# An encoder layer on one core: w_out computed by token, its two groups summed apart, the residual kept by token from the first stage on

## The chip, the cores and the metric

The kernel runs on one core of a Trainium2 chip. The metric is the device time of one execution in microseconds (us); lower is better. A core has TensorE (PE in the profile), VectorE (DVE), ScalarE (ACT), GpSimd (POOL) and SyncE (SP), which here only issues DMAs. Each engine works through its own instructions in order; semaphores tie them together. Matrix products go into PSUM, everything else lives in SBUF.

## What is computed

One layer over 256 tokens of width 2048, all in float32:

```python
h = rmsnorm(x, norm1_g);  z = h @ w_in            # columns [u | v | B | C | h_B], 1024 each
u, v = gelu(z_u), gelu(z_v);  v = layernorm(v)
y_a = u * (masked w_spatial @ v + b)              # per head, in blocks of 128 tokens
y_b = B * causal_depthwise_conv3(C * h_B)
y = concat(rmsnorm(y_a, g[:1024]), rmsnorm(y_b, g[1024:]))
x = x + y @ w_out
h2 = rmsnorm(x, norm2_g)
x = x + (silu(h2 @ w_gate) * (h2 @ w_up)) @ w_down
return rmsnorm(x, final_norm_g)
```

The width of the inner layer is 5632.

## The kernel before

**Weights.** All weights stream through once, in units of 128 x 2048 floats (1 MB), each in two halves. SP issues the DMA of a half into `raw` (`load_unit`, L105). `split` then makes two parts of it for TensorE's fast float32 form: ScalarE casts `whi<-raw` (L86), VectorE takes the rest, `wlo<-raw,whi` (L87). There are five buffers for `raw` and four for each part, so up to two units are split ahead. The activations are split in the same way, with their gain (`split_scaled`, L171 and L172), and each product is made of three terms: high x high, low x high, high x low.

**Two forms of matmul.** By token (`mm_tok`, L128 to L130): the activations are the stationary operand, 512 weight columns stream, three matmuls per token block; the result has tokens in its partitions. By feature (`mm_feat`, L136 and L137): the weights are stationary and the activations stream, high and low part side by side in one matmul of 512 columns, and a second one of 256 columns for the low weights; the result has features in its partitions, in two halves that `sum_halves` adds.

**Stages**, in the order in which PE runs them, named by their accumulators: `v` (8 units, by token), `ch` (16, by feature), `u` (8, by feature), `b` (8, by feature), `o` for w_out (16, by feature), `gu` for gate and up (88, by token), `d` for down (44, by token). x arrives by feature in `xr` (`xk(k)` is its 128 features k) and stays so. The 1/rms of norm 1 is not applied to x but afterwards, to each stage's result.

**Norms.** A row sum over features is made from squares (ScalarE) that VectorE adds up (`add_squares`), then summed over partitions by small matmuls with ones (`rstd_tokens`, `ps_n`, `ps_na`, `ps_nb`), and raised to -1/2 on GpSimd (`rstd_of`). Where the factor is needed by feature it is laid on a diagonal and spread by a further matmul (`diagonal`, `spread`: `ps_n1b`, `ps_nab`, `ps_nbb`). Groups A and B of y are scaled by theirs (`norm_group`) before they are split into `yT`. So w_out sums both groups in one accumulator; its first three accumulators take group A's half first.

**Residual.** `out_pair` adds w_out's result to `xr` by feature and splits it into `hT`. During the first eight groups of `gu`, `residual` transposes it on PE (`ps_x`) into `x_tok`, by token, which the updates of `d` (`x2_of`, L534 and L536) and the final norm need.

**The order of the work** on each engine is not that of the program text: a planner fixes it when the program is built, by the order of the text and by its own estimate of when each instruction can start. On the chip each engine then keeps to that order. A DMA also waits for an earlier one whose semaphore it takes over; there are eight in turn.

**The first loads.** SP issues `head` (the gains and x's first 128 features), then the pieces of the first unit, in quarters of 256 KB, with x's loads between them (`first_x`, `load_x`). The first quarter goes out on ScalarE's queue. While they arrive, PE runs eight matmuls on ones (`ps_warm`).

Of the kernel before, what the change touches and what calls it, by code (L numbers as in the profile page):

```python
# [16 lines left out]
P = 128  # L17
# [14 lines left out]
def trunk_layer_kernel(  # L32
# [3 lines left out]
):  # L36

# [58 lines left out]
    def load_unit(piece=HU, between=None):  # L96
# [3 lines left out]
        for h in range(2):  # L100
            raw, hi, lo = half_tiles()
            for a in range(0, HU, piece):
                s = slice(a, a + piece)
                eng = nc.scalar if first_x is between and h + a == 0 else nc.sync
                eng.dma_start(raw[:, s], u[:, h * HU + a:h * HU + a + piece])  # L105
                if between is not None:
                    between((h * HU + a) // piece)
                split(hi[:, s], lo[:, s], raw[:, s])
# [104 lines left out]
    def add_squares(acc, y, first, name):  # L213
# [3 lines left out]
        if first:  # L217
            nc.vector.tensor_tensor(acc, sq[:, 0, :], sq[:, 1, :], op=ALU.add)
        else:
            for j in range(2):  # L220
                nc.vector.tensor_tensor(acc, acc, sq[:, j, :], op=ALU.add)
# [6 lines left out]
    warm = small.tile([P, 1], F32, tag="sf", name="warm")  # L228

# [4 lines left out]
    NA = 3  # L234
    queue(w_o, [2 * i for i in range(NA)] + [2 * i + 1 for i in range(NA)] + list(range(2 * NA, KD)))
# [22 lines left out]
    def first_x(i):  # L258
        if i == 0:
            nc.scalar.copy(warm, mhalf[:, 0:1])  # L260
            nc.gpsimd.tensor_copy(xk(0), head[:, NV:])
            split_scaled(xg[0], 0, head[:, NV:], vcol(G1, 0))
        elif i == 1:
            load_x(1, 1)
# [15 lines left out]
    xsq = row("xsq")  # L280
# [24 lines left out]
    for u in range(nv):  # L305
# [13 lines left out]
        add_squares(xsq, xk(2 * u, 2), u == 0, "x")  # L319
# [12 lines left out]
    def stat_x():  # L332
        nonlocal r1, r1s, dg1
        r1 = rstd_tokens(xsq, 1.0 / D, RMS_EPS, "n1")
# [68 lines left out]
    yA = bigtile([P, KA, T], F32, "yA")  # L403
    sqA = row("sqA")
    for k in range(0, KA, 2):
# [7 lines left out]
        nc.vector.tensor_tensor(yA[:, k:k + 2, :], z, mixT[:, k:k + 2, :], op=ALU.mult)  # L413
        add_squares(sqA, yA[:, k:k + 2, :], k == 0, "ya")

    yT = units_of(2 * CA, "yT")

    def norm_group(y, rb, base):
        for k in range(0, KA, 2):
            nc.vector.tensor_tensor(y[:, k:k + 2, :], y[:, k:k + 2, :], both(rb), op=ALU.mult)  # L420
            for j in range(2):
                kk = base + k + j
                split_scaled(yT[kk // KU], kk % KU, y[:, k + j, :], vcol(GG, kk))
# [3 lines left out]
    ra, rb = [], []  # L427
    for k in range(0, KA, 2):

        acc = gemm_feat(xg, "b", (lambda: ra.append(diagonal(rstd_tokens(sqA, 1.0 / AW, 4.0 * RMS_EPS, "na"), "na")))  # L430
                        if k == 2 else None)
        z = sum_halves(acc, "b")
        if k == 2:
            rab = spread(ra[0], "na")
# [235 lines left out]
```

## Time and profile before

| | us |
|---|---|
| runs | 1074.86, 1074.89, 1075.47 (median 1074.89) |
| profiled execution | 1074.51 |
| its span | 1072.7 |
| PE busy | 1058.9 (99% of the span) |
| VectorE busy | 627.7 (59%) |
| ScalarE busy | 491.9 (46%) |
| GpSimd busy | 5.8 (1%) |
| DMA | 205 MB, 191 GB/s over the span |

The span is what the trace covers; the profiled execution's time has some 1.8 us more around it. An engine is busy while an instruction of its own runs. Matmuls are pipelined: a new one starts every 0.2 us or so although each lasts 0.4, so the distance between starts tells what one costs, not its duration. The views of the trace that are used below: busy time by stage (windows), waits (who waited for whom), the chain of work that ended last, groups of instructions by line and shape, and the order in time of single engines.

### The profile page before, as it was taken

How to read it: one execution, taken by the hardware profiler on the slowest of the kernel's cores; microseconds unless marked ns; L12 is line 12 of the kernel's file. 1: busy time of each engine (PE TensorE's matmuls, PEld its weight loads, DVE VectorE, ACT ScalarE, POOL GpSimd, SP SyncE). 2: the span in 40 equal slices, each digit the busy share in tenths (PEclk: the TensorE clock that was granted, in tenths of full speed). 3: DMA queues.
4: the chain of work that ended last, by engine and by line, in shares of the span. 5: the costliest groups of instructions: out<-in, count | busy, mean ns of one | idle time of the engine just before them, and what ended most of it. 6: DMA issues, size and time to landing. Idle time of an engine off the chain costs nothing.

```text
span 1072.7 us, 13182 instructions
## 1 busy us (share of the span) xinstructions
PE 1058.9 (99%) x5086; PEld 888.5 (83%) x5086; DVE 627.7 (59%) x760; ACT 491.9 (46%) x598; POOL 5.8 (1%) x14
## 2 busy tenths in 40 slices
PE   7999999999999999999999999999999999999996
PEld 6888888888888888888888888888888888888885
DVE  7588667778766555555455555555555445454543
ACT  7464335565554544444444444444444334343432
POOL 0000000000000000000000000000000000000000
PEclk9999999999999999999999999999999999999999
DMA  9855555555555555555555555555556555555552
GB/s 325 270 186 178 176 177 188 186 183 182 184 193 181 190 182 182 191 185 186 184 191 195 182 191 191 184 195 189 183 196 223 191 194 196 194 195 188 194 191 79
DMA packets 58415, 205.25 MB, mean 191 GB/s; under 512 B 6960, under 2 KB 7216, under 8 KB 58224
## 3 DMA queue, kind: packets, MB, share of 16 engines
q1 hardware_dynamic: 57024, 201.13, 55.9%
q10 hardware_dynamic: 1328, 3.28, 1.0%
q8 instruction: 40, 0.66, 0.2%
q14 instruction: 23, 0.19, 0.0%
HBM read 202.28 MB, written 2.10 MB: 191 GB/s over the span
## 4 chain that ended last, share of the span: by engine, by line
PE 98%; issue 1%; DMA 0%; SPq 0%; ACT 0%; DVE 0%; POOLq 0%; POOL 0%; DVEq 0%
PE gu L128 15%; PE gu L130 15%; PE gu L129 15%; PE d L129 7%; PE d L128 7%; PE d L130 7%; PE o L136 6%; PE ch L136 6%; PE o L137 3%; PE ch L137 3%; PE u L136 3%; PE b L136 3%; PE v L128 1%; PE v L129 1%; PE b L137 1%; PE u L137 1%
## 5 line engine op out<-in xcount | busy, mean ns | idle before, releaser
L87 DVE TENSOR_TENSOR wlo<-raw,whi 128x1024 fp32r<-128x1024 f32 (+1 forms) x380 | 460.7, 1213 | 414.7 <-ACT whi L86 414.2
L86 ACT CAST whi<-raw 128x1024 fp32r<-128x1024 f32 (+1 forms) x380 | 395.6, 1041 | 557.8 <-PE gu L129 275.2
L128 PE MATMUL gu<-whi,hT 128*128 128x512 f32 x704 | 276.9, 393 | 0.0
L130 PE MATMUL gu<-wlo,hT 128*128 128x512 f32 x704 | 274.4, 390 | 0.0
L129 PE MATMUL gu<-whi,hT 128*128 128x512 f32 x704 | 273.9, 389 | 0.0
L130 PEld LDWEIGHTS gu<-wlo,hT 128*128 128x128 f32 x704 | 132.1, 188 | 28.0
L129 PEld LDWEIGHTS gu<-whi,hT 128*128 128x128 f32 x704 | 132.3, 188 | 26.6
L128 PEld LDWEIGHTS gu<-whi,hT 128*128 128x128 f32 x704 | 132.2, 188 | 26.5
L128 PE MATMUL d<-whi,aT 128*128 128x512 f32 x352 | 137.0, 389 | 0.0
L130 PE MATMUL d<-wlo,aT 128*128 128x512 f32 x352 | 136.9, 389 | 0.0
L129 PE MATMUL d<-whi,aT 128*128 128x512 f32 x352 | 136.9, 389 | 0.0
L136 PE MATMUL ch<-xg,whi 128*128 128x512 f32 x256 | 90.7, 399 | 0.0
L136 PE MATMUL o<-yT,whi 128*128 128x512 f32 x256 | 90.7, 399 | 0.0
L130 PEld LDWEIGHTS d<-wlo,aT 128*128 128x128 f32 x352 | 66.1, 188 | 13.8
L128 PEld LDWEIGHTS d<-whi,aT 128*128 128x128 f32 x352 | 66.1, 188 | 13.8
L129 PEld LDWEIGHTS d<-whi,aT 128*128 128x128 f32 x352 | 66.1, 188 | 13.5
L137 PE MATMUL o<-yT,wlo 128*128 128x256 f32 x256 | 71.9, 281 | 0.0
L137 PE MATMUL ch<-xg,wlo 128*128 128x256 f32 x256 | 71.7, 280 | 0.0
L136 PEld LDWEIGHTS o<-yT,whi 128*128 128x128 f32 x256 | 48.1, 188 | 11.8
L136 PEld LDWEIGHTS ch<-xg,whi 128*128 128x128 f32 x256 | 48.1, 188 | 11.5
L137 PEld LDWEIGHTS o<-yT,wlo 128*128 128x128 f32 x256 | 48.4, 189 | 0.0
L137 PEld LDWEIGHTS ch<-xg,wlo 128*128 128x128 f32 x256 | 48.3, 189 | 0.1
(137 smaller groups left out, 735.2 us busy)
## 6 DMA issues: line engine op xcount, KB each, us to landing
raw<-in_w_gu SPq DMA_DIRECT2D x176, 512.0 KB, 3.6
raw<-in_w_d SPq DMA_DIRECT2D x88, 512.0 KB, 4.3
raw<-in_w_ch SPq DMA_DIRECT2D x32, 512.0 KB, 3.6
raw<-in_w_o SPq DMA_DIRECT2D x32, 512.0 KB, 4.4
raw<-in_w_u SPq DMA_DIRECT2D x16, 512.0 KB, 3.6
raw<-in_w_b SPq DMA_DIRECT2D x16, 512.0 KB, 3.4
raw<-in_w_v SPq DMA_DIRECT2D x12, 512.0 KB, 6.4
out<-x_tok SPq DMA_DIRECT2D x8, 256.0 KB, 2.6
```

The costliest lines, as they stand in the source:

```text
L86: nc.scalar.copy(dst_hi, src)
L87: nc.vector.tensor_tensor(dst_lo, src, dst_hi.bitcast(F32), op=ALU.subtract)
L128: nc.tensor.matmul(acc, lhsT=ah, rhs=wh, start=first, stop=False)
L129: nc.tensor.matmul(acc, lhsT=al, rhs=wh, start=False, stop=False)
L130: nc.tensor.matmul(acc, lhsT=ah, rhs=wl, start=False, stop=last)
L136: nc.tensor.matmul(acc, lhsT=wh, rhs=at[:, kk, :, :], start=first, stop=False)
L137: nc.tensor.matmul(acc[:, 0:T], lhsT=wl, rhs=at[:, kk, 0, :], start=False, stop=last)
```

## The change

1. **w_out by token.** `w_o` is laid out for the form by token. Its 2048 columns are four chunks of 512, and each chunk is computed in two parts, one for group A and one for group B, each in its own accumulator of two units; the order is A of chunks 0 and 1, B of chunks 0 and 1, then A and B of chunks 2 and 3.
2. **1/rms in the update.** y of both groups goes into `yT` without its 1/rms (`y_out`), as soon as a pair of features is done. The factor, one per token and group, is applied when a part's accumulator is added to `x_tok`. `norm_group` and two spreads go away.
3. **Residual by token from `v` on.** After every second unit of `v`, `by_token` transposes a chunk of x on PE into `x_tok`: VectorE copies it out of PSUM, ScalarE squares it there with a sum along the row (`square_part`). `residual` goes away. After w_out's update x1 is transposed back (`x1_by_feature`) and split into `hT`, after the first unit of a following part, or of `gu` for the last chunk.
4. **Row sums.** Those of x and of x1 come from `square_part` and a short sum on VectorE (`rstd_parts`), without PE. The adds of the squares of y go to GpSimd.
5. **First loads.** SP issues all of them, so the first quarter of the first unit stands behind `head`; x's first further load follows it. The copy that makes ScalarE load its table (`warm`) moves to the top.

```diff
--- before.py
+++ after.py
@@ -101,8 +103,7 @@
             raw, hi, lo = half_tiles()
             for a in range(0, HU, piece):
                 s = slice(a, a + piece)
-                eng = nc.scalar if first_x is between and h + a == 0 else nc.sync
-                eng.dma_start(raw[:, s], u[:, h * HU + a:h * HU + a + piece])
+                nc.sync.dma_start(raw[:, s], u[:, h * HU + a:h * HU + a + piece])
                 if between is not None:
                     between((h * HU + a) // piece)
                 split(hi[:, s], lo[:, s], raw[:, s])
@@ -215,10 +216,21 @@
         sq = pair(F32, "b", f"sq_{name}")
         nc.scalar.activation(sq, y, AF.Square)
         if first:
-            nc.vector.tensor_tensor(acc, sq[:, 0, :], sq[:, 1, :], op=ALU.add)
+            nc.gpsimd.tensor_tensor(acc, sq[:, 0, :], sq[:, 1, :], op=ALU.add)
         else:
             for j in range(2):
-                nc.vector.tensor_tensor(acc, acc, sq[:, j, :], op=ALU.add)
+                nc.gpsimd.tensor_tensor(acc, acc, sq[:, j, :], op=ALU.add)
+
+    def rstd_parts(parts, eps, name):
+
+        ssum = small.tile([P, NT], F32, tag="rsp", name=f"{name}_s")
+        nc.vector.tensor_reduce(ssum, parts, axis=mybir.AxisListType.X, op=ALU.add)
+        return rstd_of(ssum, 1.0, eps, name)
+
+    def square_part(dst, src):
+
+        junk = tmp.tile([P, NW], F32, tag="b", name="jk")
+        nc.scalar.activation(junk, src, AF.Square, scale=D ** -0.5, accum_out=dst)
 
 
     mhalf = const.tile([P, 2], F32, name="mhalf")
@@ -226,13 +238,15 @@
     ones = const.tile([P, P], F32, name="ones")
     nc.vector.memset(ones, 1.0)
     warm = small.tile([P, 1], F32, tag="sf", name="warm")
+    nc.scalar.copy(warm, mhalf[:, 0:1])
 
     queue(w_v)
     queue(w_ch)
     queue(w_u)
     queue(w_b)
-    NA = 3
-    queue(w_o, [2 * i for i in range(NA)] + [2 * i + 1 for i in range(NA)] + list(range(2 * NA, KD)))
+
+    o_parts = [(0, 0), (1, 0), (0, 1), (1, 1)] + [(c, h) for c in range(2, NC) for h in range(2)]
+    queue(w_o, [c * NC + 2 * h + i for c, h in o_parts for i in range(2)])
     queue(w_gu)
     queue(w_d)
 
@@ -257,11 +271,9 @@
 
     def first_x(i):
         if i == 0:
-            nc.scalar.copy(warm, mhalf[:, 0:1])
+            load_x(1, 1)
             nc.gpsimd.tensor_copy(xk(0), head[:, NV:])
             split_scaled(xg[0], 0, head[:, NV:], vcol(G1, 0))
-        elif i == 1:
-            load_x(1, 1)
         elif i == 2:
             load_x(2, 2)
             split_scaled(xg[0], 1, xk(1), vcol(G1, 1))
@@ -277,7 +289,20 @@
     make_identity(nc, ident)
 
 
-    xsq = row("xsq")
+    x_tok = const.tile([P, NT, D], F32, name="x_tok")
+    ssx = const.tile([P, NT, NC], F32, name="ssx")
+    ss1 = const.tile([P, NT, NC], F32, name="ss1")
+
+    def by_token(c):
+
+        for t in range(NT):
+            ps = pmisc.tile([P, KU, P], F32, tag="pm", name="ps_x")
+            for k in range(KU):
+                nc.tensor.transpose(out=ps[:, k, :], in_=xk(c * KU + k)[:, t * P:(t + 1) * P], identity=ident)
+            ps = ps.rearrange("p k f -> p (k f)")
+            nc.vector.tensor_copy(x_tok[:, t, c * NW:(c + 1) * NW], ps)
+            square_part(ssx[:, t, c:c + 1], ps)
+
     r1 = r1s = dg1 = r1b = r1q = None
 
     def gelu2(acc, t, dst, name):
@@ -316,7 +341,8 @@
                 for t in range(NT):
                     mm_tok(vaccs[c][:, t, :], xg[u // 2], (2 * u + k) % KU, t, w[k], c,
                            u == 0 and k == 0, u == nv - 1 and k == 1)
-        add_squares(xsq, xk(2 * u, 2), u == 0, "x")
+        if u % 2 == 1:
+            by_token(u // 2)
 
 
     wsT = bigtile([P, H, P], F32, "wsT")
@@ -331,7 +357,7 @@
 
     def stat_x():
         nonlocal r1, r1s, dg1
-        r1 = rstd_tokens(xsq, 1.0 / D, RMS_EPS, "n1")
+        r1 = rstd_parts(ssx, RMS_EPS, "n1")
         r1s = const.tile([P, NT], F32, name="r1s")
         nc.vector.tensor_scalar(r1s, r1, GELU_S, None, op0=ALU.mult)
         dg1 = diagonal(r1, "n1")
@@ -400,8 +426,15 @@
             mix(2 * (k - (KA - H // 2)))
 
 
-    yA = bigtile([P, KA, T], F32, "yA")
+    yT = units_of(2 * CA, "yT")
     sqA = row("sqA")
+
+    def y_out(y, k, acc, name):
+
+        add_squares(acc, y, k % KA == 0, name)
+        for j in range(2):
+            split_scaled(yT[(k + j) // KU], (k + j) % KU, y[:, j, :], vcol(GG, k + j))
+
     for k in range(0, KA, 2):
         z = sum_halves(gemm_feat(xg, "u"), "u")
         nc.vector.tensor_tensor(z, z, both(r1b), op=ALU.mult)
@@ -410,73 +443,57 @@
         nc.vector.scalar_tensor_tensor(b, b, 1.0, z, op0=ALU.add, op1=ALU.mult)
         nc.scalar.activation(b, b, AF.Tanh, scale=GELU_C)
         nc.vector.scalar_tensor_tensor(z, b, 1.0, z, op0=ALU.add, op1=ALU.mult)
-        nc.vector.tensor_tensor(yA[:, k:k + 2, :], z, mixT[:, k:k + 2, :], op=ALU.mult)
-        add_squares(sqA, yA[:, k:k + 2, :], k == 0, "ya")
-
-    yT = units_of(2 * CA, "yT")
-
-    def norm_group(y, rb, base):
-        for k in range(0, KA, 2):
-            nc.vector.tensor_tensor(y[:, k:k + 2, :], y[:, k:k + 2, :], both(rb), op=ALU.mult)
+        nc.vector.tensor_tensor(z, z, mixT[:, k:k + 2, :], op=ALU.mult)
+        y_out(z, k, sqA, "ya")
+
+
+    sqB = row("sqB")
+    rms = []
+    for k in range(0, KA, 2):
+
+        z = sum_halves(gemm_feat(xg, "b", (lambda: rms.append(rstd_tokens(sqA, 1.0 / AW, 4.0 * RMS_EPS, "na")))
+                                 if k == 2 else None), "b")
+        nc.vector.tensor_tensor(z, z, both(r1b), op=ALU.mult)
+        nc.vector.tensor_tensor(z, z, yB[:, k:k + 2, :], op=ALU.mult)
+        y_out(z, KA + k, sqB, "yb")
+
+
+    hT = units_of(NC, "hT")
+    turn = deque()
+
+    def x1_by_feature(c):
+        for i in range(0, KU, 2):
+            ps = pmisc.tile([P, 2, T], F32, tag="pm", name="ps_h")
             for j in range(2):
-                kk = base + k + j
-                split_scaled(yT[kk // KU], kk % KU, y[:, k + j, :], vcol(GG, kk))
-
-
-    sqB = row("sqB")
-    ra, rb = [], []
-    for k in range(0, KA, 2):
-
-        acc = gemm_feat(xg, "b", (lambda: ra.append(diagonal(rstd_tokens(sqA, 1.0 / AW, 4.0 * RMS_EPS, "na"), "na")))
-                        if k == 2 else None)
-        z = sum_halves(acc, "b")
-        if k == 2:
-            rab = spread(ra[0], "na")
-        nc.vector.tensor_tensor(z, z, both(r1b), op=ALU.mult)
-        nc.vector.tensor_tensor(yB[:, k:k + 2, :], z, yB[:, k:k + 2, :], op=ALU.mult)
-        add_squares(sqB, yB[:, k:k + 2, :], k == 0, "yb")
-        if k == 2:
-            norm_group(yA, rab, 0)
-
-
-    sq1 = row("sq1")
-    hT = units_of(NC, "hT")
-
-    def out_pair(acc, f):
-        z = sum_halves(acc, "o")
-        x1 = xk(f, 2)
-        nc.vector.tensor_tensor(x1, x1, z, op=ALU.add)
-        for j in range(2):
-            split_scaled(hT[(f + j) // KU], (f + j) % KU, x1[:, j, :], vcol(G2, f + j))
-        add_squares(sq1, x1, f == 0, "x1")
-
-    def stat_b():
-        rb.append(diagonal(rstd_tokens(sqB, 1.0 / AW, RMS_EPS, "nb"), "nb"))
-
-    def norm_b():
-        norm_group(yB, spread(rb[0], "nb", own=True), KA)
-
-    accs = [pacc.tile([P, 2, NW], F32, tag="acc", name=f"o{i}") for i in range(NA)]
-    for i in range(NA):
-        half_feat(accs[i], yT, 0, next_unit(), True, False,
-                  {(0, 6): stat_b, (1, 6): norm_b} if i == NA - 2 else None)
-    for i in range(NA):
-        half_feat(accs[i], yT, 1, next_unit(), False, True)
-        out_pair(accs[i], 2 * i)
-    for f in range(2 * NA, KD, 2):
-        out_pair(gemm_feat(yT, "o"), f)
-
-
-    x_tok = const.tile([P, NT, D], F32, name="x_tok")
+                for t in range(NT):
+                    k = c * KU + i + j
+                    nc.tensor.transpose(out=ps[:, j, t * P:(t + 1) * P], in_=x_tok[:, t, k * P:(k + 1) * P],
+                                        identity=ident)
+            for j in range(2):
+                split_scaled(hT[c], i + j, ps[:, j, :], vcol(G2, c * KU + i + j))
+
+    for n, (c, h) in enumerate(o_parts):
+        acc = pacc.tile([P, NT, NW], F32, tag="acc", name=f"o{c}_{h}")
+        for u in range(2):
+            w = next_unit()
+            for k in range(KU):
+                for t in range(NT):
+                    mm_tok(acc[:, t, :], yT[2 * h + u], k, t, w[k // 2], k % 2,
+                           u == 0 and k == 0, u == 1 and k == KU - 1)
+            if u == 0 and turn:
+                x1_by_feature(turn.popleft())
+        if n == 1:
+            rms.append(rstd_tokens(sqB, 1.0 / AW, RMS_EPS, "nb"))
+        for t in range(NT):
+            xs = x_tok[:, t, c * NW:(c + 1) * NW]
+            nc.vector.scalar_tensor_tensor(xs, acc[:, t, :], rms[h][:, t:t + 1], xs, op0=ALU.mult, op1=ALU.add)
+            if h == 1:
+                square_part(ss1[:, t, c:c + 1], xs)
+        if h == 1:
+            turn.append(c)
+
+
     aT = units_of(NF // KU, "aT")
-
-    def residual(i):
-
-        t, c = i // NC, i % NC
-        ps = pmisc.tile([P, KU, P], F32, tag="pm", name="ps_x")
-        for k in range(KU):
-            nc.tensor.transpose(out=ps[:, k, :], in_=xk(c * KU + k)[:, t * P:(t + 1) * P], identity=ident)
-        nc.scalar.copy(x_tok[:, t, c * NW:(c + 1) * NW], ps.rearrange("p k f -> p (k f)"))
 
     def gated(acc):
 
@@ -512,11 +529,10 @@
                     mm_tok(acc[:, t, :], hT[u], k, t, w[k // 2], k % 2,
                            u == 0 and k == 0, u == NC - 1 and k == KU - 1)
             if g == 0 and u == 0:
-                r2 = rstd_tokens(sq1, 1.0 / D, RMS_EPS, "n2")
+                x1_by_feature(turn.popleft())
+                r2 = rstd_parts(ss1, RMS_EPS, "n2")
             elif u == 1 and last is not None:
                 turned(*last)
-            elif u == 2 and g < NT * NC:
-                residual(g)
         last = gated(acc), g
 
 
@@ -616,6 +632,8 @@
 def _pairs(w):
 
     k, n = w.shape
+    if k == n:
+        return _token_major(w)
     t = w.reshape(k, n // (2 * P), 2, P)
     return _feature_major(t[:, :, 0].reshape(k, -1), t[:, :, 1].reshape(k, -1))
```

## Rows read from the trace of the kernel before

**Rows 1.** The page: busy time of each engine, share of the span and instructions.

```profile
PE 1058.9 (99%) x5086; PEld 888.5 (83%) x5086; DVE 627.7 (59%) x760; ACT 491.9 (46%) x598; POOL 5.8 (1%) x14
```

**Rows 2.** Waits of PE: engine, line, waited for: us in total, times, longest.

```profile
PE v L128 <- ACT xg L171: 4.4, 1, 4.4
```

**Rows 3.** Busy time by stage (v, u, o, gu): stretch, length, engines, clock, DMA.

```profile
9.24:54.50 45.26, 45.26 (x191) 37.06 (x192) 32.72 (x52) 28.11 (x42) 0.00 (x0) 1.00 0.87 307
...
149.10:194.40 45.30, 45.30 (x259) 39.32 (x259) 33.78 (x43) 22.80 (x29) 0.00 (x0) 1.00 0.55 185
...
239.90:331.12 91.22, 91.22 (x520) 79.31 (x519) 67.42 (x93) 51.01 (x71) 0.69 (x1) 1.00 0.56 187
...
331.12:824.40 493.28, 493.28 (x2234) 408.14 (x2233) 263.67 (x288) 217.60 (x253) 0.69 (x1) 1.00 0.57 190
```

**Rows 4.** The chain of work that ended last, PE's small matmuls: start, length, what.

```profile
56.29 0.34 PE ps_n L191 x4
...
60.22 0.43 PE ps_n1b L205 x2
...
112.24 0.89 PE ps_mix L373 x8
...
217.48 0.43 PE ps_nab L205 x2
...
337.92 0.52 PE ps_n L191 x4
...
348.34 0.44 PE ps_x L478 x4
```

**Rows 5.** PE in order of time where gu begins: start, length, operation.

```profile
331.12 0.40 PE L128 MATMUL gu<-whi,hT 128*128 128x512 f32 x1
...
331.83 0.40 PE L128 MATMUL gu<-whi,hT 128*128 128x512 f32 x1
```

**Rows 6.** All engines in order of time, the first ten microseconds.

```profile
1.18 0.42 SPq L105 DMA_DIRECT2D raw<-in_w_v  x1
...
1.65 0.42 SPq L254 DMA_DIRECT2D xr<-in_xt  x1
...
4.70 0.40 POOL L261 COPY xr<-head 128x256 f32<-128x256 f32 x1 [3.40 <-DMA head<-in_xt]
...
4.83 1.31 ACT L86 CAST whi<-raw 128x512 fp32r<-128x512 f32 x2 [2.17 <-DMA raw<-in_w_v]
...
6.88 0.62 ACT L86 CAST whi<-raw 128x512 fp32r<-128x512 f32 x1 [0.74 <-DMA raw<-in_w_v]
...
8.69 0.50 ACT L171 ACTIVATE xg<-head 128x256 fp32r<-128x256 f32 x1
...
9.24 0.80 PE L128 MATMUL v<-whi,xg 128*128 128x512 f32 x1 [4.38 <-ACT xg L171]
```

**Rows 7.** Groups by line and shape: count, busy us, mean ns, idle before.

```profile
L87 DVE TENSOR_TENSOR wlo<-raw,whi 128x1024 fp32r<-128x1024 f32 x372 | 455.3, 1224 | 408.8 <-ACT whi L86 408.5
...
L216 ACT ACTIVATE sq_x<-xr 128x512 f32<-128x512 f32 x16 | 9.9, 619 | 0.0
...
L172 DVE SCALAR_TENSOR_TENSOR hT<-xr,head,hT 128x256 fp32r<-128x256 f32 x16 | 7.0, 479 | 0.0
...
L221 DVE TENSOR_TENSOR xsq<-xsq,sq_x 128x256 f32<-128x256 f32 x14 | 5.9, 419 | 0.1
...
L534 DVE SCALAR_TENSOR_TENSOR x_tok<-d,n_r,x_tok 128x512 f32<-128x512 f32 x6 | 4.2, 747 | 1.9 <-PE d L130 1.9
...
L536 ACT ACTIVATE jk<-x_tok 128x512 f32<-128x512 f32 x6 | 3.8, 633 | 0.0
...
L536 ACT ACTIVATION_READ_ACCUMULATOR jk<-x_tok 128x1 f32 x10 | 1.9, 186 | 0.0
```

**Rows 8.** ScalarE in order of time, a cast late in v.

```profile
43.82 1.05 ACT L86 CAST whi<-raw 128x1024 fp32r<-128x1024 f32 x1 [1.67 <-PE v L129]
```

**Rows 9.** GpSimd in order of time, the power for r1.

```profile
57.17 0.71 POOL L184 TENSOR_TENSOR n_r<-n_v,mhalf 128x2 f32<-128x2 f32 x1 [52.08 <-DVE n_v L182]
```

## The prediction

> **What bounds the kernel now.** I read the header of the page first: PE is busy for 1058.9 of 1072.7 us, VectorE for 59%, ScalarE for 46% [rows 1]. The next view is what PE waits for: inside the work there is one wait, 4.4 us for `xg` before the first `w_v` matmul [rows 2]. Between that matmul and the last one PE never stands still, so the time is PE's start, plus what PE streams, plus a tail after the last matmul that the change doesn't touch. An edit on another engine is worth something only if it moves PE's start, changes what PE streams, or makes PE wait. The third view, busy time by stage, prices the streams: `o` (w_out) takes 91.22 us and `gu` 493.28 us, PE full in both [rows 3].
>
> **w_out by token.** Before, 256 pairs of a 512-column and a 256-column matmul. Of the 91.22 us, 0.34 and 0.43 belong to the small matmuls `ps_nb` and `ps_nbb`, which have the forms of `ps_n` and `ps_nab` [rows 4]. That leaves 90.45 us, 0.353 per pair. After, the same product is 128 triples of 512 columns, the form that `gu` has. `gu` is 704 triples in 493.28 us, less 21 blocks of `ps_a` and 8 of `ps_x` (both four fp32 transposes, 0.44) and `ps_n` at 0.52 [rows 3, 4]: 480.0 us, 0.682 per triple. 128 x 0.682 = 87.3 us. **Gain 3.2 us**, though the number of streamed columns is the same: the short matmul costs more than its columns. The other end: the first triple of `gu` after `o` took 0.71 (331.12 to 331.83) [rows 5]. If all 128 ran so, 90.9 us, a loss of 0.4. I take 0.682, the mean over 704.
>
> The page "TensorE: Matmul & The Clock Gate" of the Trainium skill, section "Back-to-back issue gap", gives N/2.4 + 2.5 ns between matmuls at full clock. By it a pair would take 325 ns and a triple 647 ns (estimates by that page), w_out would go from 83.2 to 82.9 us, and the gain would be 0.3 us. The trace shows 0.353 and 0.682, so the rule leaves out something that weighs more on the short form; the sum goes by the rows.
>
> **Small matmuls.** Removed: `ps_n` for x (0.34), the spreads `nab` and `nbb` (0.43 each), `ps_n` for x1 (0.52) [rows 4]: -1.72 us. The two row-sum groups `na` and `nb` stay. Moved: 32 transposes of x, 8 blocks at 0.44 [rows 4], from `gu` to the `v` stage; PE is full in both, so nothing is gained or lost. Added: x1 goes back to feature order, 32 transposes in 4 groups of 8. No row of before shows 8 fp32 transposes in a row; the nearest are `ps_mix`, 8 matmuls of 128 columns, 0.89, and two blocks of `ps_x`, 0.88 [rows 4]. 4 x 0.89 = +3.56 us; the two ends lie together. PE's work changes by -3.18 - 1.72 + 3.56 = **-1.34 us**, or by +2.2 at the bad end of the triples.
>
> **The start.** PE's first matmul at 9.24 waits for `xg<-head` on ScalarE (8.69), although `head` had landed by 4.70, when GpSimd copied from it. ScalarE had been given the casts of all four first raw pieces ahead of it, and waited for pieces to land between them (the third's cast begins at 6.88) [rows 6]. That order is fixed when the program is built, by a planner that evidently expects `head` late. The change puts the first raw piece behind `head` on SP's queue, so that `x`, raw pieces two to four and what follows are issued one slot later, 0.47 us, the step between SP's issues [rows 6]. The bytes ahead of piece four are the same ones, so its landing should move by little: I take 0.1 us, with bounds of 0 and 0.47. ScalarE loses one DMA issue and starts its table load earlier, which is hidden: its next work waits for a landing at 4.83 [rows 6]. If the planner leaves the order as it is, PE starts **0.1 us later**. If it moves `xg<-head` forward, PE starts earlier; these are rivals.
>
> **Row sums and the token copy.** In `v`, VectorE loses 15 adds of 0.42 (6.3 us) and gets 8 copies out of PSUM, bounded by an update out of PSUM at 0.747 (6.0 us). ScalarE loses 8 squares of 0.62 (5.0 us) and gets 8 squares with a read of the accumulator, 0.633 + 0.186 (6.6 us) [rows 7]. These wait for PE's transposes, and casts and `wlo` for the next unit queue behind them on their engines, on which PE waits in turn. The cover: a cast starts when PE frees a buffer (idle 1.67 until `PE v`, then 1.05 busy, so 2.72 us from one half unit to the next) [rows 8]. With four buffers a half is needed three halves after its cast may begin, 8.2 us, for 1.05 + 1.22 of work. Two squares and two copies (1.6 and 1.5 us) fit in the rest. Without this cover PE would pay what exceeds it, up to 1.6 us at each of four places.
>
> The longest new chain is r1. Before, it hung on `ps_n` at 56.29; now it hangs on the last squares, behind the transposes that follow `v`'s last matmul at 54.5 [rows 3, 4]. From there: transposes 0.88, two squares 1.64, a small sum (as short as the accumulator's read, 0.19), pow 0.71 [rows 7, 9]: pow ends at 57.9, and it ended at 57.88 before [rows 9]. The spread on PE, which needs it, began at 60.22, and moves to 60.8 with 0.88 added and 0.34 removed ahead of it [rows 4]. So there is as much room as before, and half a microsecond; a cast and a `wlo` that fall between (2.3 us) could take it up, and PE would wait some 0.5 us.
>
> **u, b and the GpSimd adds.** 14 adds of 128x256 go to GpSimd, which is 1% busy. Its nearest rows: a copy of that size 0.40, a two-column `pow` 0.71 [rows 6, 9]; an add should lie between 0.4 and 1.5 (the fixed cost of the one and twice the streaming of the other). `na` is asked for some 17 us after the last add, `nb` about 20 us after. VectorE in `u` gets 8 splits of 0.48 and loses 7 adds of 0.42: 33.8 to 34.7 of 45.3 us [rows 3, 7]. In `b` and `o` it is relieved, since the pass that scaled yA and yB goes away. Cost nil while VectorE has time left in `u`.
>
> The page "GPSIMD Engine Reference" of the Trainium skill, section "1. Specifications", says that GpSimd's SBUF interface is shared with VectorE instructions that have two SBUF inputs, and "4.1 Engine selection" sends elementwise adds to VectorE. That speaks against this edit; no row of before shows the two at work together.
>
> **Updates in w_out.** Per part two updates out of PSUM (0.747), for every second part two squares (0.82), and per chunk four splits on each engine [rows 7]: VectorE some 12 + 8 us and ScalarE 7 + 8 over 91 us, less than before. `d` runs the same update and square beside the same triples, and no wait of PE stands there [rows 2, 7]. New is that PE's transposes wait for the updated x_tok. They stand one unit (8 triples, 5.5 us) behind the last matmul of the part, and the two updates need 1.5 us: 4 us of cover, three `wlo` of 1.22. There are three accumulators, each needed again 22 us later.
>
> **Sum.** -1.34 + 0.1 = -1.2 us. The profiled execution took 1074.51 us (1072.7 span and 1.8 around it), 0.38 below the median of the runs, 1074.89. I take the change off the median: **1073.6 us**.
>
> **Rivals.**
> A. The planner puts `xg<-head` ahead of the fourth cast, since that piece is now issued a slot later. PE then starts after the third cast: 6.88 + 0.62 + 0.42 and a tenth, about 8.1 instead of 9.24 [rows 6]. -1.1 us more: 1072.5 (1071.5 to 1073.0). For it: `xg<-head` already stands right behind the fourth cast. Against: nothing shows where the planner expects `head`.
> B. `xg<-head` goes ahead of all casts, because raw piece one now lands after `head`. First matmul at about 6.2 (4.83 + 0.47, 0.65 for the cast, and a little): 3 us earlier, 1070.6. Against it: piece two, too, was behind `head` on one queue, and its cast still went first.
> C. Slower than before: the x1 transposes make PE wait, at the four groups after the first unit of a part. It decides where VectorE has more than three `wlo` or their like ahead of the updates. Each further one costs 1.22 us, four times 4.9: 1078.5; with half of that, 1076. For it: PE works in order, so one late update stops everything. Against: `d` shows updates with no wait behind them.
> D. GpSimd's adds hold VectorE up. In `u` 10.6 us are free for 7 adds, so it decides at 1.5 us each. At 2.2 us it costs 4.8 us: 1078.4.
> E. Long and short matmuls cost by their columns alone: the gain of 3.2 shrinks to 0.3, and the time is 1076.5. The stage means of both forms speak against it.
>
> **Chances.** Forecast 0.46 (its own range 1072.3 to 1075.0), A 0.22, B 0.10, C 0.11, D 0.04, E 0.03, others, mostly a lesser wait at r1, 0.04. A measurement of this kernel can tell about 0.2% (2.1 us) from no change. Faster by more (below 1072.7): B, two thirds of A and a fifth of the forecast, 0.34. Slower by more (above 1077.0): D, two thirds of C and a little, 0.13. Within: 0.53. The range 1071.2 to 1076.5 leaves out B and the worse part of C and D.
>
> **What would show it.** Right: triples of w_out at 0.68, `o` with three groups of transposes at about 90.3 us, `gu` some 3 us shorter, `v` 3.5 longer, and PE waiting for nothing but its start at about 9.3. A and B show as a first matmul at 8.1 or 6.2; C as waits of PE at `ps_h`; D as `wlo` in `u` longer than 1.22. The forecast is wrong if triples run at 0.71, if 8 transposes take over 1.2, or if PE waits anywhere behind the first matmul.

## The result: 1067.13 us, some 0.8% faster

The changed kernel takes 1067.13 us (median of 6 runs, 1066.75 to 1067.77). The kernel before, run beside it, takes 1075.61 (1074.86 to 1076.39). The ratio is 0.9923, with a 95% interval of 0.991 to 0.9936. Forecast were 1073.6 and a range from 1071.2 to 1076.5: the change is worth far more than foretold. The profiled execution after took 1067.12 us, its span is 1065.3, against 1074.51 and 1072.7 before.

The header of the page after, to be read against [rows 1], and what PE waits for, against [rows 2]:

```profile
PE 1055.8 (99%) x4978; PEld 882.1 (83%) x4978; DVE 619.0 (58%) x714; ACT 487.2 (46%) x596; POOL 19.3 (2%) x28
```

```profile
PE v L129 <- ACT whi L88: 0.2, 1, 0.2
```

PE works 3.1 us less, but the span is 7.4 us shorter. The wait of 4.4 us for `xg` is gone; 0.2 us for the first cast stand in its place, and this view names no other wait of PE inside the work.

Busy time by stage, after (v, ch, u, b, o, gu, d; columns as in [rows 3]); each stretch goes from a stage's first large matmul to that of the next:

```profile
5.08:53.50 48.42, 48.42 (x224) 39.19 (x225) 33.82 (x46) 30.78 (x50) 0.00 (x0) 1.00 0.91 319
53.50:147.50 94.00, 94.00 (x550) 82.29 (x548) 72.57 (x112) 45.33 (x57) 1.50 (x2) 1.00 0.54 180
147.50:191.90 44.40, 44.40 (x258) 38.81 (x258) 35.55 (x43) 25.29 (x35) 4.26 (x4) 1.00 0.56 188
191.90:236.70 44.80, 44.80 (x262) 39.23 (x261) 36.12 (x41) 25.20 (x34) 8.24 (x10) 1.00 0.56 187
236.70:327.00 90.30, 90.30 (x414) 75.05 (x413) 57.02 (x64) 44.47 (x61) 2.37 (x3) 1.00 0.56 187
327.00:817.10 490.10, 490.10 (x2206) 405.57 (x2205) 263.98 (x289) 215.45 (x249) 0.69 (x1) 1.00 0.58 191
817.10:1056.70 239.60, 239.60 (x1061) 198.42 (x1059) 116.53 (x112) 96.45 (x105) 0.55 (x1) 1.00 0.56 180
```

The same view of before for the stages that [rows 3] lacks or cuts a little shorter (v up to the start of ch, ch, b; d follows from 824.40 to 1064.00):

```profile
9.24:54.70 45.46, 45.45 (x192) 37.25 (x193) 32.72 (x52) 28.11 (x42) 0.00 (x0) 1.00 0.87 306
54.70:149.10 94.40, 94.40 (x552) 82.62 (x550) 71.29 (x109) 44.79 (x53) 1.50 (x2) 1.00 0.54 179
194.40:239.90 45.50, 45.50 (x264) 39.91 (x263) 36.92 (x53) 25.43 (x35) 0.69 (x1) 1.00 0.55 182
```

Set beside the terms of the forecast, placed in the stage where they fall:

| | before | after | difference | forecast |
|---|---|---|---|---|
| PE's first `v` matmul | 9.24 | 5.08 | -4.16 | +0.1 |
| v | 45.46 | 48.42 | +2.96 | +3.52 (8 blocks of `ps_x`) |
| ch | 94.40 | 94.00 | -0.40 | -0.34 (`ps_n`) |
| u | 45.30 | 44.40 | -0.90 | 0 |
| b | 45.50 | 44.80 | -0.70 | -0.43 (a spread) |
| o | 91.22 | 90.30 | -0.92 | -0.94 (triples, a spread, 3 groups of `ps_h`) |
| gu | 493.28 | 490.10 | -3.18 | -3.15 (`ps_x`, `ps_n`, a group of `ps_h`) |
| d | 239.60 | 239.60 | 0 | 0 |
| sum | | | -7.30 | -1.24 |

The work that the change is about, in o and gu, came out to within 0.1 us of the forecast. What the forecast lacks is the start (4.3 us) and 1.8 us in v, u, b and ch. The first microseconds, after, all engines in order of time, against [rows 6]:

```profile
0.74 0.38 SPq L257 DMA_DIRECT2D head<-in_xt  x1
1.17 0.42 SPq L106 DMA_DIRECT2D raw<-in_w_v  x1
1.64 0.42 SPq L268 DMA_DIRECT2D xr<-in_xt  x1
...
3.02 0.51 ACT L172 ACTIVATE xg<-head 128x256 fp32r<-128x256 f32 x1 [0.80 <-DMA head<-in_xt]
...
4.41 0.62 ACT L88 CAST whi<-raw 128x512 fp32r<-128x512 f32 x1 [0.88 <-DMA raw<-in_w_v]
...
5.08 0.80 PE L129 MATMUL v<-whi,xg 128*128 128x512 f32 x1 [0.21 <-ACT whi L88]
...
6.01 0.39 PE L131 MATMUL v<-wlo,xg 128*128 128x512 f32 x1
```

ScalarE now makes `xg<-head` first, at 3.02 as soon as `head` has landed, and then the first cast at 4.41. Before, it came behind four casts, at 8.69 [rows 6]. This is the order of rival B. PE starts when the first piece is cast, 4.41 + 0.62.

### The profile page after: what moved, and what is told of

Its sections match the earlier page's. It is cut to its first block, busy times and chain, and to the rows that moved or that the text cites. A ratio compares the mean times of both kernels' runs of the same rounds, so it can differ in the third digit from the quotient of the medians.

```text
span 1065.3 us, 12968 instructions
## 1 busy us (share of the span) xinstructions
PE 1055.8 (99%) x4978; PEld 882.1 (83%) x4978; DVE 619.0 (58%) x714; ACT 487.2 (46%) x596; POOL 19.3 (2%) x28
## 3 DMA queue, kind: packets, MB, share of 16 engines
q10 hardware_dynamic: 1184, 3.02, 0.8%
## 4 chain that ended last, share of the span: by engine, by line
PE 98%; issue 0%; DMA 0%; DVE 0%; ACT 0%; POOLq 0%; POOL 0%; DVEq 0%; SPq 0%
PE gu L129 15%; PE gu L131 15%; PE gu L130 15%; PE d L130 7%; PE d L129 7%; PE d L131 7%; PE ch L137 6%; PE ch L138 3%; PE b L137 3%; PE u L137 3%; PE o L129 3%; PE o L131 3%; PE o L130 3%; PE v L129 1%; PE v L131 1%; PE b L138 1%
## 5 line engine op out<-in xcount | busy, mean ns | idle before, releaser
L129 PE MATMUL o<-whi,yT 128*128 128x512 f32 x128 | 50.2, 392 | 0.0
L131 PE MATMUL o<-wlo,yT 128*128 128x512 f32 x128 | 49.9, 390 | 0.0
L130 PE MATMUL o<-whi,yT 128*128 128x512 f32 x128 | 49.8, 389 | 0.0
L137 PE MATMUL b<-xg,whi 128*128 128x512 f32 x128 | 44.6, 394 | 0.0
```

The source lines that it names most:

```text
L129: nc.tensor.matmul(acc, lhsT=ah, rhs=wh, start=first, stop=False)
L130: nc.tensor.matmul(acc, lhsT=al, rhs=wh, start=False, stop=False)
L131: nc.tensor.matmul(acc, lhsT=ah, rhs=wl, start=False, stop=last)
L137: nc.tensor.matmul(acc, lhsT=wh, rhs=at[:, kk, :, :], start=first, stop=False)
```

## Experiments: what moved the start

My theory after the result: the new order on ScalarE is worth some 5 us, the rest of the change some 3. Within the edit of the first loads there are three parts (the first raw piece on SP, the table load and warm copy ahead, and the load of `x` put one quarter earlier in the text). Four kernels take them apart; the table load was not moved alone.

**All of the change but the first loads.** The old lines of the first loads stand in the changed kernel:

```diff
-                nc.sync.dma_start(raw[:, s], u[:, h * HU + a:h * HU + a + piece])
+                eng = nc.scalar if first_x is between and h + a == 0 else nc.sync
+                eng.dma_start(raw[:, s], u[:, h * HU + a:h * HU + a + piece])
...
-    nc.scalar.copy(warm, mhalf[:, 0:1])
...
         if i == 0:
-            load_x(1, 1)
+            nc.scalar.copy(warm, mhalf[:, 0:1])
...
+        elif i == 1:
+            load_x(1, 1)
```

> The changed kernel with the first loads as they were before: the first quarter on ScalarE's queue, the x load after the second quarter, the table load in its old place. Theory (the start is worth 4.7 us: first matmul 4.2 us earlier, the first nine matmuls no longer slow, 1.3 us of it given back to waits later in v): 1067.1 + 4.7 = 1071.8 us, up to 1073 if the shorter pitch in u and b goes with it; first matmul at 9.2, the next eight 0.43 apart. Rival (the start's gain is given back in full and the rest of the change brings the 8 us): 1067 to 1068.

Measured: 1072.29 us, ratio to the kernel before 0.9969 (0.9957 to 0.9982). PE's waits:

```profile
PE v L130 <- ACT xg L173: 4.6, 1, 4.6
```

The old wait is back, and the first matmul is at 9.89, not at the expected 9.2. From ch on, each stage lasts as long as in the changed kernel, to 0.01 us: the first loads change nothing behind `v`. So the change without its first loads is worth some 3.3 us (1.9 to 4.6), and the first loads give 5.2 more (1067.13 against 1072.29).

**The first loads alone.** The kernel before with these lines turned round and nothing else.

> The kernel before with the first loads of the change, nothing else. Theory: first matmul at 5.1 us and 0.23 apart from the second on, 1075.6 - 4.7 to 6 = 1069.6 to 1070.9 us. Rival (the gain needs the rest of the change, whose v stage leaves VectorE more room): above 1073.

Measured: 1070.75 us, ratio 0.9953 (0.9938 to 0.9968). No wait of PE in `v` is left, and the first `v` matmul is at 4.98. With 0.9969 for the rest the product is 0.9922, and the whole change measured 0.9923: the two parts add up.

**The first raw piece on SP alone.**

> The kernel before with only the first quarter moved from ScalarE's queue to SP's; the x load and the table load stay in their places in the text. Theory (what counts is the order on ScalarE, and that hangs on the place of the x load): xg<-head still behind four casts, first matmul at 9.2 to 9.7, 1075.6 us within 0.5. Rival (what counts is that the quarter lands behind head): first matmul at 5 to 6, 1070 to 1072.

Measured: 1075.5 us, ratio 0.9998 (0.9989 to 1.0007). PE's wait and ScalarE in order of time:

```profile
PE v L127 <- ACT xg L170: 5.8, 1, 5.8
```

```profile
4.50 1.27 ACT L86 CAST whi<-raw 128x512 fp32r<-128x512 f32 x2 [2.28 <-DMA raw<-in_w_v]
...
9.57 0.62 ACT L86 CAST whi<-raw 128x512 fp32r<-128x512 f32 x1 [1.85 <-DMA raw<-in_w_v]
10.10 0.50 ACT L170 ACTIVATE xg<-head 128x256 fp32r<-128x256 f32 x1
```

Four casts still come first, and the first matmul is at 10.65, later than the expected 9.2 to 9.7. `head` could be read at 3.08 and the first piece was cast at 4.50, so the piece did land behind `head`, as rival B asks, and the order stayed. The queue of the first piece, on which the prediction's rivals A and B hung the order, does not set it.

**The place of one load alone.** One line of the kernel before is moved:

```diff
         if i == 0:
+            load_x(1, 1)
             nc.scalar.copy(warm, mhalf[:, 0:1])
...
-        elif i == 1:
-            load_x(1, 1)
```

> The kernel before with only the x load moved in the text, from behind the second quarter to behind the first; the first quarter stays on ScalarE's queue. Theory (order): xg<-head runs first on ScalarE at 4.6, then the first cast, first matmul at about 5.8, 3.4 us earlier; PE idle for 0.9 us between warm-up and first matmul instead of 4.4. 1071 to 1072.5 us. Rival (the queue counts): 1075.6 and a first matmul at 9.2.

Measured: 1070.17 us, ratio 0.9949 (0.9934 to 0.9963), under the expected 1071 to 1072.5, with the first matmul at 5.22 instead of 5.8. ScalarE and PE in order of time:

```profile
4.15 0.51 ACT L171 ACTIVATE xg<-head 128x256 fp32r<-128x256 f32 x1 [1.48 <-DMA head<-in_xt]
4.56 0.60 ACT L86 CAST whi<-raw 128x512 fp32r<-128x512 f32 x1
...
5.22 0.79 PE L128 MATMUL v<-whi,xg 128*128 128x512 f32 x1 [0.35 <-ACT whi L86]
```

This line alone turns the order and brings the whole gain of the start. The first raw piece still goes out on ScalarE's queue here, `head` lands a microsecond later than in the changed kernel (4.15 against 3.02), and PE starts only 0.14 later, since it waits for the cast. Why the planner answers so to the place of a load is not shown by any run.

## Experiments: why an earlier start gives more than its microseconds

In the kernel before, the matmuls that follow the wait are slow: from 9.24 to 13.01 there are eight steps in 3.77 us (0.72, 0.59, five of 0.43 and 0.32), and later steps are 0.23. PE before:

```profile
10.98 0.63 PE L128 MATMUL v<-whi,xg 128*128 128x512 f32 x1
11.41 0.63 PE L129 MATMUL v<-whi,xg 128*128 128x512 f32 x1
...
13.01 0.40 PE L130 MATMUL v<-wlo,xg 128*128 128x512 f32 x1
```

In the changed kernel the third step is fast already. Is it PE's idle time of 4.4 us, or are the operands late?

**A longer warm-up in the kernel before.** `WARM` goes from 8 to 24, so PE is busy until 8.4.

> The kernel before with 24 warm-up matmuls instead of 8 and nothing else; ScalarE's order, and with it the start of the first v matmul (9.2 us), stays. In the trace of the kernel before the first nine v matmuls stand some 0.43 us apart (9.24 to 13.0) and the later ones 0.23; in the runs where PE hardly idles between the warm-up and v the pace is 0.23 from the third on. Theory that PE's idle time of 4.4 us behind the warm-up costs a slow start: with PE busy until about 8.6 the nine stand 0.23 apart, and the time is some 1.8 us under the kernel before (ratio about 0.9983). Rival: the slow matmuls come from their operands, pieces cast one by one while VectorE and ScalarE are full: they stay slow, and the time stays within 0.3 us.

Measured: 1073.14 us, ratio 0.9983 (0.9974 to 0.9993). PE in order of time:

```profile
9.77 0.73 PE L128 MATMUL v<-whi,xg 128*128 128x512 f32 x2 [1.35 <-ACT xg L171]
10.49 0.50 PE L129 MATMUL v<-whi,xg 128*128 128x512 f32 x1
10.82 0.40 PE L130 MATMUL v<-wlo,xg 128*128 128x512 f32 x1
11.06 0.39 PE L128 MATMUL v<-whi,xg 128*128 128x512 f32 x1
```

PE still waits for the same `xg`, for 1.35 us, but from 10.82 on the steps are 0.23 to 0.24. The stage takes 43.9 us instead of 45.46.

**A shorter warm-up in the changed kernel.** `WARM` goes from 8 to 1; PE idles for 3.0 us ahead of `v`.

> The changed kernel with 1 warm-up matmul instead of 8. Theory of the idle time: PE idles from about 1.5 to 5.1, the first v matmuls stand 0.43 apart for some 3.8 us, which costs up to 1.85 us; part of it is covered, since the matmuls from 9.7 to 12.6 wait for pieces of weights anyway (their gaps are .33 to .39, some 1.4 us in all): between 0.4 and 1.85 us over the changed kernel, 1067.5 to 1069.0. Rival, pace set by the operands: no change, 1067.1.

Measured: 1068.07 us, 0.94 above the changed kernel. PE in order of time, then two stretches of it by busy time:

```profile
4.91 0.79 PE L129 MATMUL v<-whi,xg 128*128 128x512 f32 x1 [3.03 <-ACT whi L88]
...
9.34 0.63 PE L130 MATMUL v<-whi,xg 128*128 128x512 f32 x1
```

```profile
5.50:9.77 4.27, 4.27 (x12) 3.26 (x10) 2.44 (x6) 2.35 (x5) 0.00 (x0) 1.00 0.89 262
10.38:14.26 3.88, 3.88 (x18) 3.19 (x17) 3.69 (x7) 3.42 (x8) 0.00 (x0) 1.00 1.04 403
```

The operands are as early as in the changed kernel, and yet ten steps from 5.50 to 9.77 take 0.427 each: 512 columns at 1.2 per ns, the pace of the lower of TensorE's two clock levels (1.2 and 2.4 GHz). From 10.38 to 14.26 there are 17 steps of 0.228. The Trainium skill, "TensorE: Matmul & The Clock Gate", section "Back-to-back issue gap", gives N/1.2 ns between matmuls for the slow clock, 427 for 512 columns; the row agrees.

The column of the granted clock (the third from the end) reads 1.00 in both stretches, but of the slow one it says nothing: the trace's own records of the clock begin at 10.09 us here, at the full level, and the column counts the time ahead of them as full. In the kernel before they begin at 12.86, in the changed one at 5.88, with the long warm-up at 4.70, each time where the steps turn fast. A later run with the old order on ScalarE, the kernel before with one matmul more (below), holds more of them: the level rises at 4.54, near the end of the warm-up, falls at 7.96, while PE waits for `xg`, and rises again at 14.78. Over its first ten `v` steps the column shows the lower level:

```profile
9.81:14.53 4.72, 4.72 (x10) 3.43 (x11) 4.64 (x11) 4.49 (x10) 0.00 (x0) 0.50 1.03 379
```

So the slow pace is the clock's, and PE's idle time ahead of `v` prolongs it: behind the same eight warm-up matmuls the steps turn fast at 5.88 where `v` follows after 0.2 us, and at 12.86 where it follows after 4.4. The kernel with one warm-up matmul changes both the idle time and the work ahead of it, and can't tell the two apart.

Set against steps of 0.2275, the first eight cost the kernel before 3.77 - 8 x 0.2275 = 1.95 us, and the first two cost the changed one 0.93 - 0.455 = 0.48 (from 5.08 to 6.01). That is 1.5 us gained. Not all of the 1.95 is the clock: with the long warm-up the first three steps, 9.77 to 10.82, still lose 0.37, so the idle time is worth some 1.6 us, by which the two `v` stages differ. In part the gain is given back. PE after, a little later:

```profile
9.73 0.50 PE L129 MATMUL v<-whi,xg 128*128 128x512 f32 x1
10.07 0.40 PE L130 MATMUL v<-whi,xg 128*128 128x512 f32 x1
10.46 0.50 PE L131 MATMUL v<-wlo,xg 128*128 128x512 f32 x1
...
12.59 0.40 PE L129 MATMUL v<-whi,xg 128*128 128x512 f32 x1
```

The nine steps from 9.73 to 12.59 take 2.86 us instead of 2.05: PE now runs into pieces of weights that have just landed and are still being cast. In v that leaves 4 x 0.87 for the transposes - 1.47 + 0.81 = +2.8, of 2.96 measured.

**Later loads of x behind the weights.** In the loop of `v` the changed kernel issues a step's load of `x` ahead of that step's weights:

```diff
-            if u + 2 < nv:
-                load_x(2 * u + 4, 2)
             load_unit(HU if u else NW,
...
                                    vcol(G1, 2 * u + 2 + i // m)))
+            if u + 2 < nv:
+                load_x(2 * u + 4, 2)
```

> The changed kernel with the later loads of x in the loop of v issued behind the weights of the step instead of ahead of them. In the trace of the changed kernel matmuls from 9.7 to 12.6 stand .33 to .39 apart instead of .23, each behind a piece of weights that is cast as it lands. If those waits are for weights that x loads pushed back, they shrink: some 0.7 us (0.3 to 1.4) under the changed kernel, 1066.4. Rival: bandwidth is used up either way (300 to 435 GB/s in these 16 us), the wait goes to x and comes back later: same, 1067.1, or up to 1 us slower.

Measured: 1066.69 us, 0.44 below the changed kernel; ratio to the kernel before 0.9919 (0.9904 to 0.9934). In its trace the steps from 9.62 to 12.57 are .22 to .23: the waits are gone. Some of the 0.8 is lost at the start: its first five steps, 4.96 to 7.09, take 2.13 us, 1.0 more than at .2275, where the changed kernel lost 0.5. Three of them take .427, and the records of the clock begin at 6.86. In the last kernel of the next section, with the same order of loads, they begin at 4.75 and no step takes .427: as far as two executions tell, the loss belongs to the execution, not to the loads. It is the fastest of these kernels, but its interval and that of the changed kernel overlap almost wholly.

## Experiments: why u became faster

No edit in u takes work from PE, and yet the stage is 0.9 us shorter. PE after, where u begins; two steps make a pair:

```profile
147.88 0.40 PE L137 MATMUL u<-xg,whi 128*128 128x512 f32 x1
148.12 0.28 PE L138 MATMUL u<-xg,wlo 128*128 128x256 f32 x1
148.23 0.39 PE L137 MATMUL u<-xg,whi 128*128 128x512 f32 x1
```

All 128 pairs of u stand 0.347 apart here (44.40/128), and 0.354 before (45.30/128 [rows 3]). It is not that VectorE is less busy; it is more (35.55 us against 33.78). Taken in eights, pairs run at either of two paces in every kernel, .354 or .346, and change between them only at small matmuls (`ps_mix`, `ps_na`, the spread for r1).

**One small matmul more ahead of u**, a column whose result is not used, in the kernel before and in the changed kernel:

```diff
             mix(2 * (k - (KA - H // 2)))
+    ps = pmisc.tile([P, NW], F32, tag="pm", name="ps_dummy")
+    for _ in range(1):
+        nc.tensor.matmul(ps[:, 0:1], lhsT=ones, rhs=ones[:, 0:1], start=True, stop=True)
```

> The kernel before with one matmul of one column more between the last matmul of the convolution stage and the first of u (its result is not used). In the kernel before all 128 pairs of u stand .354 apart, in the changed kernel .346, and the pace changed in both only at places where small matmuls stand between pairs. Theory that the small matmul shifts how the pairs fall, whatever it computes: u goes to .346, its stage is 44.4 instead of 45.3 us. Rival, the pace belongs to the data or the buffers of a stage: u stays at .354 and 45.3 us.

> The changed kernel with the same one matmul of one column between the convolution stage and u. Theory of the shift: u goes from .346 to .354, 44.4 to 45.3 us, and so b, which has no small matmul before it. Rival, the pace belongs to the stage's data or buffers: u stays at .346 and 44.4 us.

**Two of them** in the kernel before (`range(2)`):

> The kernel before with two matmuls of one column more between the convolution stage and u. With one more, u went from .354 to .346 us a pair (45.3 to 44.4 us), and in the changed kernel from .346 to .354. Theory that each small matmul turns the pace once: with two, u is back at .354 and 45.3 us. Rival, any insertion settles the pace anew and two are no more than another draw: u may be at .346, 44.4 us.

The first matmul of each pair of u: duration min/median/max in ns, first and last start; after, then the kernel before with one more, the changed kernel with one more, the kernel before with two more:

```profile
L137 PE MATMUL u<-xg,whi x128: 392/395/473, 147.5 to 191.6; 128*128 128x512 f32 x128
```

```profile
L136 PE MATMUL u<-xg,whi x128: 392/395/475, 150.5 to 194.6; 128*128 128x512 f32 x128
```

```profile
L137 PE MATMUL u<-xg,whi x128: 395/398/478, 147.6 to 192.6; 128*128 128x512 f32 x128
```

```profile
L136 PE MATMUL u<-xg,whi x128: 395/398/481, 150.7 to 195.6; 128*128 128x512 f32 x128
```

127 steps take 44.1, 44.1, 45.0 and 44.9 us. One matmul of one column makes u of the old kernel as fast as the new one's, and u of the new kernel as slow as the old one's; two leave it as it was. So the 0.9 us in u belong neither to the moved adds nor to the row sums; they hang on which small matmuls PE runs ahead of the stage. In times: the changed kernel with one more took 1069.07 (u and b both at the slow pace, +0.9 each), the kernel before with one more 1075.34 and with two 1076.16 (one run each; with one more, b and w_out lost 0.1 and 0.2 again behind `ps_na`).

**Can it be used?** The kernel with the loads of x behind the weights gets one such matmul behind the first 32 pairs of ch.

```diff
         else:
+            if k == 1:
+                ps = pmisc.tile([P, NW], F32, tag="pm", name="ps_dummy")
+                nc.tensor.matmul(ps[:, 0:1], lhsT=ones, rhs=ones[:, 0:1], start=True, stop=True)
             acc = gemm_feat(xg, "ch")
```

> The changed kernel with the later loads of x behind the weights and one matmul of one column more in the convolution stage, behind its first 32 pairs. There some 128 pairs follow up to the first ps_mix, at .354 in all kernels so far. Theory that one small matmul turns the pace: they run at .346, which gives 128 x .0075 = 0.96 us less 0.15 for the matmul; what the pace is behind the next small matmuls is not foretold (u is worth 0.9 us, and so is b): 1065.9 if they stay, 1067.8 if u and b go to .354. Rival: these 128 pairs stay at .354, 1066.8.

Measured: 1068.11 us, 1.4 more than without it. The 128 pairs stayed at .354, and u went to it, too:

```profile
L137 PE MATMUL u<-xg,whi x128: 393/398/478, 146.9 to 191.9; 128*128 128x512 f32 x128
```

The theory that each small matmul turns the pace falls here; the rival, that they stay, held for ch, though not its time of 1066.8. An insertion settles the pace of what comes later, in a way that I can't foretell. What sets it stays open.

## Experiment: the adds of squares on GpSimd

`nc.gpsimd.tensor_tensor` in `add_squares` becomes `nc.vector.tensor_tensor` again, in the changed kernel:

> The changed kernel with the adds of the squares on VectorE again, as in the kernel before. My prediction took the move to GpSimd for worth nothing either way, since VectorE has time in u and b. Theory: within 0.2% of the changed kernel (1067.1, give or take 0.5), GpSimd's busy time falls from 19.3 to some 6 us. Rival D of the prediction (adds of GpSimd hold VectorE up): 0.5 to 2 us faster, VectorE's operations of u shorter than in the changed kernel.

Measured: 1067.17 us against 1067.13, ratio to the kernel before 0.9921 (0.9904 to 0.9937): no difference, and from u to gu each stage is as long as in the changed kernel, to 0.01 us. But part of rival D's mechanism is there. The adds on GpSimd, after (busy us, mean ns):

```profile
L222 POOL TENSOR_TENSOR sqA<-sqA,sq_ya 128x256 f32<-128x256 f32 x6 | 6.1, 1024 | 28.0 <-ACT sq_ya L217 27.8
```

VectorE's splits of y, min/median/max in ns, after, and with the adds on VectorE:

```profile
L173 DVE SCALAR_TENSOR_TENSOR yT<-z_u,head,yT x8: 470/960/965, 169.3 to 203.5; 128x256 fp32r<-128x256 f32 x8
L173 DVE SCALAR_TENSOR_TENSOR yT<-z_b,head,yT x8: 471/859/965, 208.8 to 243.2; 128x256 fp32r<-128x256 f32 x8
```

```profile
L173 DVE SCALAR_TENSOR_TENSOR yT<-z_u,head,yT x8: 478/479/480, 169.9 to 203.9; 128x256 fp32r<-128x256 f32 x8
L173 DVE SCALAR_TENSOR_TENSOR yT<-z_b,head,yT x8: 477/478/482, 209.1 to 243.6; 128x256 fp32r<-128x256 f32 x8
```

While GpSimd adds, 14 of the 16 splits on VectorE take 0.85 to 0.97 us, up to twice their 0.48. `wlo` does not grow, which was D's sign: beside an add for up to 0.65 us it keeps 1.22 to 1.23 us, and there the add takes longer, 1.24 us, against 0.80 or 0.81 beside splits alone. It costs nothing here, since VectorE has some 9 us to spare in each of these stages. The Trainium skill, "GPSIMD Engine Reference", section "1. Specifications", says that GpSimd shares its SBUF interface with VectorE instructions of two SBUF inputs, as these splits are; the rows agree. Which of the two engines waits they don't settle: beside `wlo`, which also has two SBUF inputs, it is GpSimd.

## Why the prediction was wrong

**The start, the step that failed.** The prediction said "If the planner leaves the order as it is, PE starts 0.1 us later", and took that for the likeliest. The order did not stay. The case stood among the rivals, as B, with a chance of 0.10, and it was argued from the wrong edit: whether the first raw piece lands after `head`. That edit alone does nothing (ratio 0.9998). The load of `x`, of which I said only that it is issued a slot later, turns the order alone (0.9949). It was not even issued later: at 1.64, and at 1.65 before [rows 6]. From the trace of before, the planner's answer could not be read; and one line in another place was enough to change it; the reason I gave for the old order, that the planner expects `head` late, was itself read from that order.

**B's own price was short as well**, 1070.6 for 1067.13. It put the start at 6.2, from the old landing of the first piece plus a slot. The cast began at 4.41, not at 5.30: `head` and the piece, issued one behind the other, both came earlier than before, when ScalarE's queue sent the piece alongside. That is 1.1 us. It also left out the slow steps behind PE's idle time, which stood in the trace of before, right behind the 4.4 us of [rows 2]; 1.5 us, of which 0.8 came back as waits for pieces. And u and b gave 1.2 that no row foretold.

**The median of before.** Six profiled executions whose ScalarE keeps the old order have their first `v` matmul at 9.24, 9.8, 9.8, 9.9, 10.0 and 10.7. The one on which the forecast rests is the earliest. Each of those starts needs four pieces to have landed, so it moves with the slowest. Where PE was idle ahead of `v`, the rise of the clock moves as well: 12.86 in that execution, 13.2 to 16.1 in four others. This fits a difference of 8.5 us between the medians and of 7.4 between the two profiled executions; no run shows that it is the whole reason.

**What held.** w_out by token: (90.30 - 3 x 0.87 - 0.34)/128 = 0.682 us a triple, as forecast, not the 0.71 of the bad end, and not the estimate by columns alone (rival E). Eight transposes take 0.87 or 0.88, for 0.89 taken. PE's small matmuls after, from the chain of work:

```profile
17.56 0.87 PE ps_x L301 x8
...
58.62 0.43 PE ps_n1b L206 x2
...
275.52 0.87 PE ps_h L470 x8
```

PE waits nowhere at `ps_h`, so rival C did not come about: the updates take 0.75 each and are long done. The spread for r1 stands at 58.62 without a wait; its diagonal on VectorE was ready by 57.4. The row sums on ScalarE and the copies on VectorE (0.69 each) cost nothing, as costed. The adds on GpSimd took 0.80 to 1.24 us, inside the bounds of 0.4 and 1.5.

## What to carry to other kernels

Where a planner orders an engine's work, the order of the old trace is no constant: price an edit near a stretch of dependent first work with the order free, down to the earliest landing, and give that case real weight. Price a late start with what follows it: idle time ahead of the first matmuls kept the next ones at the lower clock here, some 1.6 us beyond the wait. And before a gain of 1 us in a long stage is put down to an edit, compare the distance of its matmuls: here a stage's pace moved by 2% through one matmul of one column.

## What was not expected of the hardware

- Pairs of a 512- and a 256-column matmul run at one of two paces, .354 or .346 us, for long stretches, and change only at small matmuls. What sets the pace is open.
- After one warm-up matmul and 3.0 us without work PE ran eleven steps at .43 to .59 instead of .23. The profile's column of the granted clock reads 1.00 there only because the trace has no record of the clock before 10.09 us.
- GpSimd's adds stretched VectorE's splits of the same size from .48 to up to .97 us, while `wlo` on VectorE stretched the adds, from .80 to 1.24.
- `head`, issued ahead of the first raw piece on one queue, could be read at 2.97 to 3.10 in eight executions; with that piece on a second queue, at 4.15 to 4.70 in six.
